# Projection stage of a hybrid backbone step: rotation tables and heads' Newton steps on GpSimd, half of the modulated tiles on ScalarE, pooling products one group sooner

## The chip, the cores and the metric

The kernel runs on one core of a Trainium2 chip. The metric is the device time of one execution in microseconds, as the median of several runs. The engines are called as in the profile: PE (TensorE, matrix products), PEld (its weight loads), DVE (VectorE), ACT (ScalarE), POOL (GpSimd) and SP (SyncE, which here only issues DMAs).

## What is computed

Two layers over 2048 latent tokens and 256 prompt tokens of width 1024. In each layer one input projection feeds three branches, attention, a short gated convolution and a multi-scale pooling, and one output projection joins them:

```python
xn = _rmsnorm(x, norm_g) * (1 + scl) + shift
proj = xn @ w_in
q, k, v, z_a, h_c, b_c, c_c, z_c, u_p, z_p = jnp.split(proj, SPLIT_IDX, axis=-1)
q = _rmsnorm(q.reshape(B, n, N_HEADS, HEAD_DIM), q_g)
k = _rmsnorm(k.reshape(B, n, N_KV_HEADS, HEAD_DIM), k_g)
...
q = _apply_rope(q, angs)
k_all = jnp.concatenate([_apply_rope(k, angs), ctx_k], axis=1)
...
attn = _attend(q, k_all, v_all) * jax.nn.silu(z_a)
conv = b_c * _short_conv(c_c * h_c, conv_w, conv_b) * jax.nn.silu(z_c)
pool = _pool_mix(u_p, pool_w, pool_scale) * jax.nn.silu(z_p)
out = jnp.concatenate([attn, conv, pool], axis=-1) @ w_out
return x + gate * out, k, v
```

The rotation applies to latent tokens alone; the prompt has none. `w_in` has 2816 columns: 512 of q, 128 of k, 128 of v, 512 of `z_a`, and six groups of 256.

## The kernel before

The kernel has two stages per layer: `phase_a`, the projection, and `phase_b`, attention and output projection. The change touches `phase_a` alone. It keeps about single precision by splitting each operand of a product into a rounded high part and the rest: `xh` and `xl` of the tokens, `wh` and `wl` of the weights, and three products for each, `wh*xh`, `wl*xh`, `wh*xl`. ACT makes the high parts by a cast; DVE and POOL share the low parts, a subtraction each (`split_w`, line 422: odd quarters of a weight tile on POOL, even ones on DVE).

The tokens of a layer are three blocks in the first half (two of 512 latent tokens and the prompt's 256) and two of 512 in the second. `norm_block` scales the tokens of a block by the root of their mean square. `tr_block` (line 431) transposes them on PE, eight tiles `trx` for the eight slices of the width; DVE makes of each the modulated tile `xf` (times `modA` plus `modB`), ACT the cast `xh`, POOL the difference `xl`. Only for the first block of layer 1 does ACT make every second `xf`. PE needs `xf` for the next transpose too, since two buffers hold the transposed tiles.

Over the blocks runs a sequence of weight tiles of 256 columns: two for q, one for kv, then the `rest` (z_a; h and c of the convolution; its b and z; u and z of the pooling), each as a loop over the blocks. While PE multiplies one tile, the next is split.

A q unit is 256 tokens times four heads. ACT copies the products to `raw` and squares them to `sq`, DVE sums the squares of each head to `hs` (line 500); POOL multiplies `raw` by the cosine table to `ra` (line 511), DVE by the sine table, four times into `sq` (line 520), and POOL adds both (line 181). When the block's last unit is there, `head_roots` (line 534) takes the inverse root of all `hs` of the block by three Newton steps, and `head_scale` (line 525, instruction on line 529) multiplies `ra` by it. Only then can PE transpose the heads (`trq`, `trk`), and ACT and DVE split them into `qh`, `ql` or `kh`, `kl`, which are stored. A block of 512 tokens has 16 roots per token row for q and 8 for kv; the prompt has half of them.

`newton_parts` (line 145) is a list of twelve instructions on DVE: `nt_v` (line 154), a shift `nt_t` (155) and a subtraction `nt_y` (157) on the bits as a start value, and then three times lines 151, 152 and 153. There are 15 of these for heads in each layer.

The rotation tables `trig` hold cosines and signed sines for 16 groups of 128 tokens. `small_loads` (line 375) multiplies them by the norm gains, once for q (g = 0) and once for k (g = 1), five instructions for each, all on DVE; in layer 0 it first multiplies `gains` by 8.

The pooling branch: `pool_out` sums windows on DVE (line 724 and on), ACT casts the difference to `dh`, POOL makes `dl`, and PE multiplies both with the group weights (`pmix`, lines 755 to 757). DVE scales the result to `po` (line 758), ACT casts it to `mh` and POOL subtracts `ml`, which are stored.

The order of instructions on each engine is written out by hand: every engine runs its queue in the order of the program, and waits are semaphores on tiles. Three helpers interleave work: `fine` runs one small function after every second k-slice of the products, `hook` runs after each unit, and `after(f, n)` (line 464) runs `f` at the n-th hook from now. The products of the pooling go through it:

```python
after(post, PR['po'])
```

`PR['po']` is 5. A hook is one unit on PE, 24 products of 512 columns for a latent block of the rest. `wg`, `wgh` and `wgl` are the split of the gated output weights, which fills the gaps of DVE, ACT and POOL in the later units.

Of the kernel before, what the change touches and what calls it, by code (L numbers as in the profile page):

```python
# [9 lines left out]
F32 = mybir.dt.float32  # L10
F32R = mybir.dt.float32r
F16 = mybir.dt.float16
I32 = mybir.dt.int32
# [17 lines left out]

PR = {'oa': 6, 'po': 5, 'q1': 3, 'q2': 5, 's0': 14, 's0p': 7, 'q1p': 0, 'ma': 3, 'mb': 1, 'd0': 3, 'd1': 2, 'dp': 1,
# [63 lines left out]
def hybrid_step(ctx: ExitStack, tc: tile.TileContext, A, O):  # L96
# [63 lines left out]
    def newton(pool, src, n, tag, eps):  # L160
        y, fns = newton_parts(pool, src, n, tag, eps)
        for f in fns:
            f()
        return y

    late = [[], []]
# [101 lines left out]
    def phase_a(l, xs_src, xp_src, nxt):  # L268


        with ExitStack() as st, ExitStack() as left:
# [102 lines left out]

            def small_loads():
                if l == 0:
                    nc.vector.tensor_scalar(out=gains, in0=gains, scalar1=8.0, scalar2=None, op0=ALU.mult)
                for g in range(2):
                    gn = gains[:, l, g:g + 1, :]
                    nc.vector.tensor_tensor(out=trig[:, g, 0], in0=trig[:, 1, 0], in1=gn.to_broadcast([128, 16, 64]),  # L380
                                            op=ALU.mult)
                    for c in range(2):
                        for f in range(2):
                            o, e = 32 * c + 16 * f, 32 * c + 16 * (1 - f)
                            nc.vector.tensor_tensor(out=trig[:, g, 1, :, o:o + 16], in0=trig[:, 1, 1, :, o:o + 16],
                                                    in1=gn[:, :, e:e + 16].to_broadcast([128, 16, 16]), op=ALU.mult)

# [42 lines left out]

            def tr_block(b, first=False):

# [5 lines left out]
                def one(k):  # L438
# [4 lines left out]
                    mA, mB = (m[:, l, k, b.cond:b.cond + 1] for m in (modA, modB))  # L443
                    if first and l and k % 2:
                        nc.scalar.activation(out=f[:, 0:b.n], in_=ps[:, 0:b.n], func=AF.Identity, scale=mA, bias=mB)
                    else:
                        nc.vector.tensor_scalar(out=f[:, 0:b.n], in0=ps[:, 0:b.n], scalar1=mA, scalar2=mB,
                                                op0=ALU.mult, op1=ALU.add)
# [85 lines left out]
            def head_roots(nh, b):  # L534
                m = b.n // 256 * 2 * nh
                b.r = newton(sm, b.ss[:, 0:m], m, "rh", 64 * EPS)

# [345 lines left out]
            for si, (half, kind, c) in enumerate(seq):  # L883
# [52 lines left out]
                def block(b, bi, kind, c, w):  # L936
# [10 lines left out]
                    elif kind == "za":  # L947
                        for m in range(2):
# [4 lines left out]
                            if si == 0 and (bi, m) == (1, 1):  # L953
                                if l:
                                    trig_loads()
                                    small_loads()
                                pool_loads()
# [43 lines left out]
                for bi, b in enumerate(order):  # L1001
                    if l == 0 and si == 0 and bi == 0:
                        fine.add([lambda i=i: split_w(w_next, i, 4) for i in range(4)])
                        nsplit[0] = 4
                        fine.add([lambda: norm_block(blocks[0][1]), small_loads])
                        fine.add([lambda: jobs_early.extend(jobs_at[1]())])
# [3 lines left out]
                        fns = [lambda i=i, f=f: (f(), others[i]() if i < len(others) else None)  # L1010
                               for i, f in enumerate(tr_block(blocks[0][1]))]
                        fine.add([lambda: None] * PR['e8'] + fns)
                        block(b, bi, seq[1][1], seq[1][2], w_next)
# [6 lines left out]
                    if si in (0, len(CH)) and bi + 1 < len(blocks[half]):  # L1020
                        fns = tr_block(blocks[half][bi + 1])
                        others = norm_parts(blocks[0][2]) if PR['np'] and l and si == 0 and bi == 0 else ()
# [806 lines left out]
```

## Time and profile before

| | us |
|---|---|
| median of 3 runs | 3221.98 (3221.13 to 3222.83) |
| the profiled execution | 3220.74 |
| its span, first to last instruction | 3219.0 |
| projection stage of layer 0 (with the start) | 0 to 672 |
| attention and output projection of layer 0 | 672 to 1620 |
| projection stage of layer 1 | 1620 to 2265 |
| attention and output projection of layer 1 | 2265 to 3219 |

The mean granted PE clock is 0.986 of full speed. In the rows, a time is the start in microseconds from the span's start, the number behind it how long it took (a row of several instructions has one sum), and a bracket at the end says how long the engine stood idle before and which instruction ended it. The profile's rows name shapes as partitions x elements. Matmuls overlap, so the distance of two starts is what one takes.

### The profile page before, as it was taken

The page shows a single profiled execution, that of the slowest core. Times are in us where ns is not written, and L with a number is a line of the kernel's source. Part 1 is how long each engine was busy: PE and PEld are TensorE (multiplying, and loading weights), DVE is VectorE, ACT ScalarE, POOL GpSimd, SP SyncE. Part 2 cuts the span into 40 slices and gives each one's busy share as a digit, 9 for nine tenths or more (in the row PEclk, how much of TensorE's full clock was granted, in tenths as well). Part 3 has the DMA queues.
Part 4 walks back from the last instruction along what each step waited for, and adds up shares of the span by engine and source line. Part 5 has one row for each costly group of instructions (what it writes and reads, how often), then busy time and mean ns, then how long its engine had stood idle before and what let it go on. Part 6 is the DMA issues. An engine that isn't in the chain of part 4 may idle for free.

```text
span 3219.0 us, 48084 instructions
## 1 busy us (share of the span) xinstructions
PE 3072.0 (95%) x17642; PEld 2438.0 (76%) x17642; DVE 2310.4 (72%) x3728; ACT 1833.5 (57%) x2634; POOL 2015.0 (63%) x1290
## 2 busy tenths in 40 slices
PE   6899999999999999999989999999899999999997
PEld 5788888766677777777769888988667777677775
DVE  5656575357888888888767555843778888888886
ACT  3323332237777777777742323331677887787785
POOL 2424462226888888888833334621578888898885
PEclk9999999999999999999999999999999999999999
DMA  7245744445234241323333455434623432342444
GB/s 249 90 129 188 246 143 136 131 132 156 74 120 119 62 128 56 105 79 110 127 138 100 148 165 193 131 99 120 171 80 117 123 102 76 90 132 83 130 145 149
DMA packets 371970, 408.40 MB, mean 127 GB/s; under 512 B 33428, under 2 KB 319640, under 8 KB 370968
## 3 DMA queue, kind: packets, MB, share of 16 engines
q1 hardware_dynamic: 371736, 405.33, 40.8%
q8 instruction: 140, 2.29, 0.3%
q14 instruction: 94, 0.77, 0.1%
HBM read 285.69 MB, written 119.55 MB: 126 GB/s over the span
## 4 chain that ended last, share of the span: by engine, by line
PE 69%; DVE 16%; ACT 4%; DMA 4%; issue 4%; POOL 2%; SPq 1%; DVEq 0%; ACTq 0%; POOLq 0%
PE mx L1158 7%; PE st L1198 6%; PE st L1197 6%; PE pv L1243 6%; PE rest L640 6%; PE rest L642 6%; PE rest L641 6%; PE pv L1250 4%; DVE mr L1159 4%; DVE Z L1229 3%; PE op L1376 3%; PE op L1377 3%; PE op L1378 3%; PE lc L1278 2%; PE qkv L481 2%
## 5 line engine op out<-in xcount | busy, mean ns | idle before, releaser
L181 POOL TENSOR_TENSOR pl<-P,ph 128x1024 f16<-128x1024 f32 (+2 forms) x594 | 1236.1, 2092 | 285.1 <-ACT ph L1209 256.6
L1159 DVE TENSOR_REDUCE mr<-mx 128x1 f32<-128x512 f32 x1024 | 696.2, 685 | 271.4 <-PE mx L1158 265.8
L1207 ACT ACTIVATE P<-st 128x1024 f32<-128x1024 f32 x576 | 636.0, 1104 | 286.3 <-PE st L1198 281.0
L1229 DVE TENSOR_REDUCE Z<-P 128x152 f32<-128x912 f32 (+2 forms) x576 | 695.7, 1208 | 6.6 <-ACT P L1207 5.5
L1209 ACT ACTIVATE ph<-st 128x1024 f16<-128x1024 f32 x584 | 591.3, 1012 | 0.0
L1158 PE MATMUL mx<-KH,T 128*128 128x512 f32 x1024 | 487.2, 477 | 34.5 <-DVE mr L1159 20.0
L640 PE MATMUL rest<-xh,wh 128*128 128x512 f32 (+1 forms) x1264 | 477.6, 378 | 2.2 <-ACT wh L427 2.2
L642 PE MATMUL rest<-xh,wl 128*128 128x512 f32 (+1 forms) x1264 | 469.3, 371 | 7.0 <-DVE wl L429 7.0
L641 PE MATMUL rest<-xl,wh 128*128 128x512 f32 (+1 forms) x1264 | 469.1, 371 | 2.0 <-POOL xl L181 2.0
L1197 PE MATMUL st<-T,KH 128*128 128x512 f32 x1152 | 462.5, 401 | 2.3 <-ACT ph L1209 2.3
L1198 PE MATMUL st<-T,KL 65*128 65x512 f32 x1152 | 460.4, 400 | 0.0
L1243 PE MATMUL pv<-ph,V 128*128 128x512 f16 x1152 | 351.3, 387 | 2.2 <-ACT P L1207 1.8
L1158 PEld LDWEIGHTS mx<-KH,T 128*128 128x128 f32 x1024 | 195.4, 191 | 195.2 <-DVE mr L1159 87.6
L429 POOL TENSOR_TENSOR wl<-wf,wh 128x512 fp32r<-128x512 f32 x88 | 124.0, 1409 | 277.8 <-ACT wh L427 256.7
L642 PEld LDWEIGHTS rest<-xh,wl 128*128 128x128 f32 x1264 | 240.3, 190 | 49.9 <-DVE wl L429 8.5
L640 PEld LDWEIGHTS rest<-xh,wh 128*128 128x128 f32 x1264 | 240.9, 191 | 46.2 <-issue 5.5
L641 PEld LDWEIGHTS rest<-xl,wh 128*128 128x128 f32 x1264 | 240.9, 191 | 40.4 <-POOL xl L181 3.3
L1198 PEld LDWEIGHTS st<-T,KL 65*128 65x128 f32 x1152 | 219.3, 190 | 48.0
L481 PE MATMUL qkv<-wl,xh 128*128 128x256 f32 x864 | 247.5, 287 | 7.2 <-DVE wl L429 4.2
L1197 PEld LDWEIGHTS st<-T,KH 128*128 128x128 f32 x1152 | 220.0, 191 | 41.3 <-ACT ph L1209 4.8
L480 PE MATMUL qkv<-wh,xh 128*128 128x256 f32 x864 | 250.9, 290 | 0.0
L482 PE MATMUL qkv<-wh,xl 128*128 128x256 f32 x864 | 246.5, 285 | 0.0
(234 smaller groups left out, 5533.8 us busy)
## 6 DMA issues: line engine op xcount, KB each, us to landing
wo<-woH SPq DMA_DIRECT2D x144, 256.0 KB, 3.7
wo<-woL SPq DMA_DIRECT2D x144, 256.0 KB, 5.1
wf<-in_w_in SPq DMA_DIRECT2D x50, 512.0 KB, 6.2
wa<-in_w_ada SPq DMA_DIRECT2D x24, 1024.0 KB, 6.7
wf<-in_w_in SPq DMA_DIRECT2D x19, 1024.0 KB, 5.6
woH<-wgh SPq DMA_DIRECT2D x64, 256.0 KB, 2.5
woL<-wgl SPq DMA_DIRECT2D x64, 256.0 KB, 2.5
T<-qH SPq DMA_DIRECT2D x128, 128.0 KB, 4.4
```

The source lines that it names most:

```text
L181: nc.gpsimd.tensor_tensor(out=out, in0=a, in1=b, op=op)
L640: nc.tensor.matmul(out=ps[:, 0:b.n], lhsT=wh[:, k, ms], rhs=b.h[:, k, :], start=(k == 0), stop=False)
L641: nc.tensor.matmul(out=ps[:, 0:b.n], lhsT=wh[:, k, ms], rhs=b.l[:, k, :], start=False, stop=False)
L642: nc.tensor.matmul(out=ps[:, 0:b.n], lhsT=wl[:, k, ms], rhs=b.h[:, k, :], start=False, stop=(k == KD - 1))
L1158: nc.tensor.matmul(out=ps, lhsT=u.T1[:, q * 128:(q + 1) * 128], rhs=u.KH[u.g][:, c * 512:(c + 1) * 512])
L1159: nc.vector.reduce_max(out=mr[:, q, c:c + 1], in_=ps, axis=AX.X)
L1197: nc.tensor.matmul(out=ps[:, i, :], lhsT=u.KH[u.g][:, kt], rhs=u.T1, start=True, stop=False)
L1198: nc.tensor.matmul(out=ps[:, i, :], lhsT=u.KL[u.g][0:65, kt], rhs=u.T2, start=False, stop=True)
L1207: nc.scalar.activation(out=P, in_=ps, func=AF.Exp, scale=0.125)
L1209: nc.scalar.activation(out=ph, in_=ps, func=AF.Exp, scale=0.125)
L1229: nc.vector.tensor_reduce(out=z[:, c], in_=u.P[grp][:, 0:ns, c, :].rearrange("p s n t -> p n s t"), axis=AX.XY, op=ALU.add)
L1243: nc.tensor.matmul(out=u.po, lhsT=u.V[u.g][:, 2 * j + i, :], rhs=ph[:, i, :], start=(j == 0 and i == 0), stop=False)
```

## The change

Four edits, all of `phase_a`:

1. `small_loads` takes the half g and its instructions go to POOL. In layer 0 the first half stays where the whole stood (behind the norm of block 1), the second goes behind the transposes of block 1. In layer 1 the first half stays and the second comes four hooks later.
2. `head_roots` uses `newton_gp`: the three start instructions stay on DVE (with the scale 1.0 in the first), the three steps are four POOL instructions each. It holds for the 15 Newtons of the heads in each layer; the norm of the tokens keeps the old one.
3. In layer 0, blocks 1 and 2 of the first half have every second `xf` made by ACT (`beside`).
4. `PR['po']` is 4: the pooling products come one hook sooner.

DVE has 299 instructions fewer, POOL 381 more, ACT 8 more; PE has the same.

```diff
-PR = {'oa': 6, 'po': 5, 'q1': 3, 'q2': 5, 's0': 14, 's0p': 7, 'q1p': 0, 'ma': 3, 'mb': 1, 'd0': 3, 'd1': 2, 'dp': 1,
+PR = {'oa': 6, 'po': 4, 'q1': 3, 'q2': 5, 's0': 14, 's0p': 7, 'q1p': 0, 'ma': 3, 'mb': 1, 'd0': 3, 'd1': 2, 'dp': 1,
...
+    def newton_gp(pool, src, n, tag, scale, eps):
+
+        v = pool.tile([128, n], F32, tag="nt_v", name="nt_v")
+        y = pool.tile([128, n], F32, tag=tag, name="nt_y")
+        t = pool.tile([128, n], F32, tag="nt_t", name="nt_t")
+        ps, ts = nc.gpsimd.tensor_scalar, nc.vector.tensor_scalar
+        step = [lambda: padd(t, y, y, ALU.mult), lambda: padd(t, t, v, ALU.mult),
+                lambda: ps(out=t, in0=t, scalar1=-0.5, scalar2=1.5, op0=ALU.mult, op1=ALU.add),
+                lambda: padd(y, y, t, ALU.mult)]
+        return y, [lambda: ts(out=v, in0=src, scalar1=scale, scalar2=eps, op0=ALU.mult, op1=ALU.add),
+                   lambda: ts(out=t.bitcast(I32), in0=v.bitcast(I32), scalar1=1, scalar2=None,
+                              op0=ALU.logical_shift_right),
+                   lambda: ts(out=y.bitcast(I32), in0=t.bitcast(I32), scalar1=-1.0, scalar2=float(0x5F3759DF),
+                              op0=ALU.mult, op1=ALU.add)] + step * 3
...
-            def small_loads():
-                if l == 0:
-                    nc.vector.tensor_scalar(out=gains, in0=gains, scalar1=8.0, scalar2=None, op0=ALU.mult)
-                for g in range(2):
-                    gn = gains[:, l, g:g + 1, :]
-                    nc.vector.tensor_tensor(out=trig[:, g, 0], in0=trig[:, 1, 0], in1=gn.to_broadcast([128, 16, 64]),
-                                            op=ALU.mult)
-                    for c in range(2):
-                        for f in range(2):
-                            o, e = 32 * c + 16 * f, 32 * c + 16 * (1 - f)
-                            nc.vector.tensor_tensor(out=trig[:, g, 1, :, o:o + 16], in0=trig[:, 1, 1, :, o:o + 16],
-                                                    in1=gn[:, :, e:e + 16].to_broadcast([128, 16, 16]), op=ALU.mult)
+            def small_loads(g):
+
+                if l == 0 and g == 0:
+                    nc.gpsimd.tensor_scalar(out=gains, in0=gains, scalar1=8.0, scalar2=None, op0=ALU.mult)
+                gn = gains[:, l, g:g + 1, :]
+                padd(trig[:, g, 0], trig[:, 1, 0], gn.to_broadcast([128, 16, 64]), ALU.mult)
+                for c in range(2):
+                    for f in range(2):
+                        o, e = 32 * c + 16 * f, 32 * c + 16 * (1 - f)
+                        padd(trig[:, g, 1, :, o:o + 16], trig[:, 1, 1, :, o:o + 16],
+                             gn[:, :, e:e + 16].to_broadcast([128, 16, 16]), ALU.mult)
...
-                    if first and l and k % 2:
+                    if (l and first or not l and beside) and k % 2:
                         nc.scalar.activation(out=f[:, 0:b.n], in_=ps[:, 0:b.n], func=AF.Identity, scale=mA, bias=mB)
...
-                b.r = newton(sm, b.ss[:, 0:m], m, "rh", 64 * EPS)
+                b.r, fns = newton_gp(sm, b.ss[:, 0:m], m, "rh", 1.0, 64 * EPS)
+                for f in fns:
+                    f()
...
                                 if l:
                                     trig_loads()
-                                    small_loads()
+                                    small_loads(0)
+                                    after(lambda: small_loads(1), 4)
                                 pool_loads()
...
-                        fine.add([lambda: norm_block(blocks[0][1]), small_loads])
+                        fine.add([lambda: norm_block(blocks[0][1]), lambda: small_loads(0)])
...
-                               for i, f in enumerate(tr_block(blocks[0][1]))]
-                        fine.add([lambda: None] * PR['e8'] + fns)
+                               for i, f in enumerate(tr_block(blocks[0][1], beside=True))]
+                        fine.add([lambda: None] * PR['e8'] + fns + [lambda: small_loads(1)])
...
-                        fns = tr_block(blocks[half][bi + 1])
+                        fns = tr_block(blocks[half][bi + 1], beside=not si)
```

In the changed file the lines from 163 on stand 15 to 17 further down: `head_scale` is 543, `xf` 461, the rotation's product 525, `padd` 196, `po` 774.

**DVE, layer 0, the first q Newton and what follows it** (a row is line, operation, output <- inputs, shape, count). Before, from the last sine products to the prompt's tiles:

```order
L520 TENSOR_TENSOR sq<-raw,trig 128x8x16 x4
L154 TENSOR_SCALAR nt_v<-hs 128x16
L155 TENSOR_SCALAR nt_t<-nt_v 128x16
L157 TENSOR_SCALAR nt_y<-nt_t 128x16
L151 SCALAR_TENSOR_TENSOR nt_t<-nt_y 128x16
L152 TENSOR_TENSOR nt_t<-nt_t,nt_v 128x16
L153 SCALAR_TENSOR_TENSOR nt_y<-nt_t,nt_y 128x16
...
L529 TENSOR_TENSOR ra<-ra,nt_y 128x512 x2
L447 TENSOR_SCALAR xf<-trx,modA,modB 128x256 x8
```

Now:

```order
L534 TENSOR_TENSOR sq<-raw,trig 128x8x16 x4
L175 TENSOR_SCALAR nt_v<-hs 128x16
L176 TENSOR_SCALAR nt_t<-nt_v 128x16
L178 TENSOR_SCALAR nt_y<-nt_t 128x16
L543 TENSOR_TENSOR ra<-ra,nt_y 128x512 x2
L461 TENSOR_SCALAR xf<-trx,modA,modB 128x256 x4
```

The nine steps are gone from this queue, `head_scale` follows the start value directly, and four of the prompt's eight tiles have left.

**POOL, the same place.** Before, from the last unit's rotation on:

```order
L511 TENSOR_TENSOR ra<-raw,trig 128x512
L181 TENSOR_TENSOR ra<-ra,sq 128x512
L181 TENSOR_TENSOR xl<-xf,xh 128x256 x8
L391 MEMSET pwf 128x128 x2
L511 TENSOR_TENSOR ra<-raw,trig 128x512
```

Now:

```order
L525 TENSOR_TENSOR ra<-raw,trig 128x512
L196 TENSOR_TENSOR ra<-ra,sq 128x512
L196 TENSOR_TENSOR nt_t<-nt_y 128x16
L196 TENSOR_TENSOR nt_t<-nt_t,nt_v 128x16
L173 TENSOR_SCALAR nt_t<-nt_t 128x16
L196 TENSOR_TENSOR nt_y<-nt_y,nt_t 128x16
...
L196 TENSOR_TENSOR trig<-trig,gains 128x1024
L196 TENSOR_TENSOR trig<-trig,gains 128x16x16 x4
L196 TENSOR_TENSOR xl<-xf,xh 128x256 x8
```

Twelve small steps and then five table rows stand between the rotation's sum and the prompt's `xl`. In the other Newtons no table follows, but the rows that followed the sum before: a `wl`, a rotation, or the prompt's gains.

**DVE, layer 1, the first pooling unit.** Before, from its scaling on:

```order
L740 SCALAR_TENSOR_TENSOR s<-s,kc,rb 128x256
L429 TENSOR_TENSOR wl<-wf,wh 128x512
L758 SCALAR_TENSOR_TENSOR po<-pmix,cols,rb 128x508 x2
L429 TENSOR_TENSOR wl<-wf,wh 128x512
L689 COPY carry<-rb 128x16 x2
```

Now:

```order
L756 SCALAR_TENSOR_TENSOR s<-s,kc,rb 128x256
L774 SCALAR_TENSOR_TENSOR po<-pmix,cols,rb 128x508 x2
L443 TENSOR_TENSOR wl<-wf,wh 128x512 x2
L774 SCALAR_TENSOR_TENSOR po<-pmix,cols,rb 128x256
L705 COPY carry<-rb 128x16 x2
```

The scaling of the products stands ahead of both quarters of the weight tile instead of between them, and that of the prompt ahead of the second pooling unit.

## Rows read from the trace of the kernel before

**Rows 1.** The page's busy time by engine, share of the span, instructions

```profile
PE 3072.0 (95%) x17642; PEld 2438.0 (76%) x17642; DVE 2310.4 (72%) x3728; ACT 1833.5 (57%) x2634; POOL 2015.0 (63%) x1290
```

**Rows 2.** Windows: us, busy us of PE, PEld, DVE, ACT, POOL, clock, DMA, GB/s

```profile
0.00:672.00 672.00, 620.63 (x3854) 529.52 (x3854) 367.77 (x784) 200.25 (x370) 243.64 (x207) 0.98 0.52 165
...
1620.00:2265.00 645.00, 616.53 (x3566) 538.96 (x3565) 379.56 (x733) 207.81 (x382) 241.63 (x203) 0.98 0.43 135
```

**Rows 3.** PE's timeline: start, us, engine, line, tiles, [idle before <-releaser]

```profile
71.66 0.90 PE L441 MATMUL trx<-kc,x 128*128 128x128 f32 x3 [5.35 <-DVE xf L447]
...
94.55 0.44 PE L441 MATMUL trx<-kc,x 128*128 128x128 f32 x2 [2.98 <-DVE xf L447]
...
148.66 0.85 PE L230 MATMUL aps<-wa,sT 128*32 128x256 f32 x12 [2.22 <-DVE ql L558]
...
486.01 1.08 PE L230 MATMUL aps<-wa,sT 128*32 128x256 f32 x8 [3.68 <-DVE ql L558]
...
1758.12 0.63 PE L551 MATMUL trq<-kc,ra 128*128 128x128 f32 x4 [1.58 <-DVE ra L529]
```

**Rows 4.** The windows of two stretches of 4 us, columns as in group 2

```profile
72.00:76.00 4.00, 4.00 (x22) 4.00 (x21) 2.04 (x6) 3.38 (x7) 3.42 (x4) 0.54 0.02 4
92.00:96.00 4.00, 1.45 (x9) 1.22 (x10) 3.76 (x11) 1.33 (x4) 0.99 (x2) 1.00 0.00 0
```

**Rows 5.** DVE's timeline ahead of the wait of 5.35 us

```profile
62.83 0.29 DVE L377 TENSOR_SCALAR gains<-gains 128x256 f32<-128x256 f32 x1
...
69.21 0.67 DVE L500 TENSOR_REDUCE hs<-sq 128x8 f32<-128x512 f32 x1
```

**Rows 6.** POOL's timeline in the same stretch

```profile
64.53 1.33 POOL L511 TENSOR_TENSOR ra<-raw,trig 128x512 f32<-128x512 f32 x1 [8.60 <-DVE trig L380]
```

**Rows 7.** DVE's timeline, one 16-wide heads' Newton and `head_scale`

```profile
142.00 0.17 DVE L154 TENSOR_SCALAR nt_v<-hs 128x16 f32<-128x16 f32 x1
...
142.61 1.28 DVE L151 SCALAR_TENSOR_TENSOR nt_t<-nt_y 128x16 f32<-128x16 f32 x1
143.93 1.22 DVE L152 TENSOR_TENSOR nt_t<-nt_t,nt_v 128x16 f32<-128x16 f32 x1
...
146.71 1.29 DVE L529 TENSOR_TENSOR ra<-ra,nt_y 128x512 f32<-128x512 f32 x2
```

**Rows 8.** POOL's timeline beside that Newton

```profile
143.82 1.30 POOL L429 TENSOR_TENSOR wl<-wf,wh 128x512 fp32r<-128x512 f32 x1
```

**Rows 9.** POOL's timeline, small dependent steps in the last stage

```profile
3182.74 0.20 POOL L181 TENSOR_TENSOR nt_t<-or 128x4 f32<-128x4 f32 x1
...
3184.69 0.20 POOL L181 TENSOR_TENSOR or<-or,nt_t 128x4 f32<-128x4 f32 x1
```

**Rows 10.** POOL's timeline, long subtractions of the pooling branch

```profile
268.97 2.65 POOL L181 TENSOR_TENSOR dl<-s,dh 128x1016 fp32r<-128x1016 f32 x1 [6.48 <-ACT dh L744]
...
1831.31 2.34 POOL L181 TENSOR_TENSOR dl<-s,dh 128x1016 fp32r<-128x1016 f32 x1 [3.92 <-ACT dh L744]
...
1859.24 2.37 POOL L181 TENSOR_TENSOR dl<-s,dh 128x1016 fp32r<-128x1016 f32 x1 [7.94 <-ACT dh L744]
...
1880.24 2.34 POOL L181 TENSOR_TENSOR ml<-po,mh 128x1016 fp32r<-128x1016 f32 x1
```

**Rows 11.** PE's timeline at the first products of three pooling units

```profile
275.93 0.40 PE L755 MATMUL pmix<-dh,pwh 128*128 128x508 f32 x1
276.17 0.40 PE L756 MATMUL pmix<-dl,pwh 128*128 128x508 f32 x1
...
1833.70 0.50 PE L756 MATMUL pmix<-dl,pwh 128*128 128x508 f32 x1 [1.87 <-POOL dl L181]
...
1863.73 0.39 PE L756 MATMUL pmix<-dl,pwh 128*128 128x508 f32 x1
```

**Rows 12.** PE's timeline, two waits in a weight split

```profile
1880.59 0.50 PE L640 MATMUL rest<-xh,wh 128*128 128x512 f32 x1 [1.24 <-ACT wh L427]
...
1883.19 0.50 PE L642 MATMUL rest<-xh,wl 128*128 128x512 f32 x1 [1.87 <-DVE wl L429]
```

More of the change, by code (lines that the diff above doesn't have):

```diff
@@ L429, in split_w, with tr_block @@
                 eng.tensor_tensor(out=lo[:, s], in0=v, in1=h[:, s], op=ALU.subtract)
-            def tr_block(b, first=False):
+            def tr_block(b, first=False, beside=False):
                 nt = b.n // 128
```

## The prediction, made blind

> **What bounds the kernel now.** I read the page first: TensorE (PE) is busy for 95% of the span, VectorE (DVE) for 72%, GpSimd (POOL) for 63% [rows 1]. So a gain must come out of PE's idle time, or out of a clock that is not granted, in the stretches that the change touches. Those are the two projection stages, one per layer. In the windows by stage PE is busy 620.63 of 672 us in the first and 616.53 of 645 us in the second [rows 2]; the first includes the start-up, which the change leaves alone. Then I read PE's timeline there for rows with an idle time, and the engine behind each. They are short and have a pattern: PE waits 5.35 us for `xf` from DVE, 2.98 us for `xf`, 2.22 and 3.68 us for `ql`, 1.58 us for `ra` [rows 3], and each time DVE had just run either the rotation tables or a heads' Newton. Last come the timelines of DVE and POOL at these places.
>
> **Tables of layer 0.** DVE makes them in one go: `gains` starts at 62.83, and the next work, the sum `hs`, at 69.21 [rows 5]: 6.4 us in which the tiles `xf` that PE needs stand behind them. POOL is idle for 8.60 us until 64.53 [rows 6], so its first half of the tables fits there. The price on POOL: a 128x1016 subtraction takes 2.34 us [rows 10], a 128x512 one 1.30 [rows 8], so 128x1024 about 2.4 and 128x256 about 0.65, by estimate; a half of the tables is 2.4 + 4 x 0.65 = 5.0 us. They are not free for DVE: ahead of 62.83 it runs the small steps of the token norm and the scaling of x, and a DVE instruction that meets a POOL one waits to its end (two steps of the 0.17-us kind take 1.28 and 1.22 beside POOL's work [rows 7]). In the worst case the norm meets all five POOL rows and is put off by some 4 of their 5 us, and the gain on DVE is only 6.4 - 4 = 2.4. In the best case the whole stall of 5.35 goes, and with it the clock: the granted clock is 0.54 from 72 to 76 and 1.00 again at 92 to 96, right after a stall of 2.98 [rows 4], so 4 x (1 - 0.54) = 1.8 us more, 7.2 in all. A middle value is nearer the best, as POOL has 8.60 us for 5.0: **-6**. What is late next is `xl`, which POOL makes from these tiles; that does not change.
>
> **The second half of the tables** is put behind the first Newton on POOL, ahead of the prompt's eight `xl`, and DVE's two `head_scale` (line 529, 1.29 us for both [rows 7]) are ready at the moment when POOL starts a 2.4-us table. If POOL starts first, DVE waits 2.4 us, then 0.65 behind a small one, and the prompt's `xf`, for which PE already waits 2.98 us, come that much later: 3.1, and with the Newton's own delay (below) more. If DVE starts first it is 0. POOL has no semaphore to wait for there, so I take the first: **+3.5** (0 to 5). In layer 1 the same block stands ahead of a `wl` and an `ra`. PE has no idle time there before, so some of it is slack: **+1** (0 to 4.5). The tables that DVE gives up in layer 1 lie where PE does not wait: 0. The eight `xf` that go to ScalarE are 0 too: it is mostly idle there, and PE waits for the first tile, which stays on DVE.
>
> **Newton.** Before: three start steps and nine small steps on DVE, of 0.17 us where nothing is in their way (the first [rows 7]). At 142.00 the whole thing takes 4.71 us to `head_scale` at 146.71, of which 2.1 are two waits for POOL's `ra` and `wl` [rows 7]. After: three steps on DVE, then twelve on POOL. POOL's small dependent steps exist once in this trace, in the last stage: from 3182.74 to 3184.69 lie seven intervals [rows 9], 1.95 / 7 = 0.28 us each; twelve are 3.35. (Those are 128x4, these 128x16: at 0.20 us most of a step is not the elements.) The third start step ends with POOL's `ra` in any case (that wait of about 1.2 stays), so a 16-wide Newton takes about 0.5 + 1.2 + 3.35 + 0.1 = 5.1 us from start to `head_scale`, against 4.71 here. DVE's order has `head_scale` right behind the third start step, so DVE is not free for other work meanwhile: 299 instructions fewer, but the queue stands. Behind the last Newton step POOL has a `wl` ready (1.30 [rows 8]) that ran *during* the Newton before; started first, it holds `head_scale` for 1.3 us. So the site costs 0.4 to 1.7 us. There are some eight such sites where PE already waits behind a Newton; four are shown [rows 3]. At 0.7 each: **+5.5** (0 to 12).
>
> *A rule of the Trainium skill against the trace.* The rows above show that two steps of 0.17 us took as long as the POOL instruction beside them. "SBUF — State Buffer", section "Who interferes with whom", says that VectorE and GpSimd hold one port pair exclusively for a whole instruction, whoever starts first; the trace agrees. By the same skill's "GPSIMD Engine Reference", section "Engine selection", elementwise work on two inputs belongs on VectorE, being about 2x slower on GpSimd, which speaks against this change; by that factor the nine steps of 0.17 would be 3.1 us, where the rows give 3.35 for twelve, so the sum stays.
>
> **Pooling products one group sooner.** A group is 24 matmuls at 0.23 to 0.24 us from start to start [rows 11], 5.6 us. In layer 1 PE already waits 1.87 us for `dl` at the first one [rows 11], whose POOL instruction runs from 1831.31 to 1833.65 [rows 10]; nothing in the change makes that chain earlier. So PE comes 5.6 us sooner and waits 7.5: +5.6 and a clock drop of 1.8, **+7.4**. At the next one PE reads `dl` (done 1861.61) from 1863.73 on; 5.6 sooner it would wait 3.5, less about 2, since `po` and `wl` in front of that chain also come sooner: +1.6. In layer 0 the same: `dl` done at 271.62, read at 276.17 [rows 10, 11]: 5.6 - 4.55 = +1. In return `po`, `mh`, `ml` come before the split of the next weight tile and no longer between its parts. Before, `ml` (2.34 us from 1880.24 [rows 10]) held DVE's `wl`, and PE waited 1.24 and 1.87 us [rows 12], followed by slower matmuls worth about as much as the drop above: -4.9. Sum 7.4 + 1.6 + 1 - 4.9, **+5** (0 if the chain gives way by as much, 11 if the return stays out).
>
> **The sum** is -6 + 3.5 + 1 + 5.5 + 5 = +9 us, against the profiled execution of 3220.74 us (span 3219.0): 3229.7. That execution stands 1.2 us under the median of 3221.98, so the forecast is 3231. With all terms at their lower ends it is -7.2, so 3215; at their upper ends -2.4 + 5 + 4.5 + 12 + 11 = +30, so 3252.
>
> **The rivals.**
> - *Faster: a quick hand-back.* Place: the end of each Newton. If DVE's `head_scale` starts ahead of POOL's next instruction, and the POOL steps hide the waits that DVE had within the Newton (1.28 + 1.22 at 142 [rows 7]), a site goes from 4.7 to 4.4 or less. It decides from 4.4 us on, counted from the first Newton step to `head_scale`: then Newton and tables cost nothing (0 for +3.5, +1, +5.5), the tables give 7.2, and `dl`, behind a less crowded DVE, is some 4 us sooner, so the products cost 1: -6 to -10, about **3214**. For it: DVE is the releaser of nearly all of PE's waits here. Against it: `head_scale` stands directly behind the start steps.
> - *No difference.* The change shifts waits from one engine to the other without changing when `head_scale` ends (in this sense it does not do what it says), and 0 for Newton and +3 for the products meet -6 and +3.5: **3222**.
> - *GpSimd becomes the bound.* POOL's `wl` halves come 3.35 us later at each Newton and 5 us more behind the tables. If PE waits for those as it does for DVE's, every term is at its upper end: **3248**.
>
> **How the numbers follow.** Forecast, slower by about 9: 0.38. GpSimd as the bound: 0.08. No difference: 0.27. Faster: 0.27. A measurement of this kernel tells 0.2%, 6.4 us, from no change; so faster 0.27, same 0.27, slower 0.46. The range runs from 3212, just under the faster rival's 3214, to 3246, just under the bound one's 3248; what is left out is a gain of over 10 us (0.1) and the bound case (0.08).
>
> **What would show it.** In the changed kernel's profile: PE's wait of 5.35 near 71 us gone or under 3 (tables); PE's wait before the prompt's transposes over 5 us, with POOL on a 128x1024 table during it (second half); `head_scale` some 5 us after the first Newton step and over 1 us long where a `wl` runs on POOL; a wait of 6 to 8 us for `dl` at the first product of layer 1, and none near 1880. It would be wrong if the products' chain in layer 1 is sooner than now, or if DVE gets to `head_scale` first: then the time falls under 3222.

## The result and the profile after

| | before | after |
|---|---|---|
| median of 4 runs each, us | 3221.56 (3220.26 to 3222.83) | 3269.27 (3266.92 to 3275.66) |
| ratio of the times, 95% interval | | 1.0153 (1.0140 to 1.0165) |
| the profiled execution and its span | 3220.74, 3219.0 | 3266.92, 3265.1 |
| mean granted PE clock | 0.986 | 0.979 |

The change costs 47.7 us. The forecast was 3231, the range 3212 to 3246: the sign was right, the size was five times too small, and the range missed it.

The page's busy time of the changed kernel, columns as in [rows 1], and the windows by stage, columns as in [rows 2]; the last two windows are of 4 us each.

```profile
PE 3088.1 (95%) x17642; PEld 2450.9 (75%) x17642; DVE 2271.2 (70%) x3429; ACT 1838.2 (56%) x2642; POOL 2117.1 (65%) x1671
```

```profile
0.00:697.00 697.00, 626.05 (x3855) 532.76 (x3856) 349.33 (x633) 204.69 (x378) 293.79 (x398) 0.97 0.51 159
1644.00:2281.00 637.00, 598.11 (x3439) 524.35 (x3439) 339.75 (x558) 202.91 (x372) 293.32 (x393) 0.97 0.42 132
...
96.00:100.00 4.00, 2.48 (x8) 2.09 (x9) 1.96 (x4) 2.44 (x6) 4.00 (x6) 0.50 0.00 0
...
504.00:508.00 4.00, 3.02 (x21) 1.75 (x22) 3.97 (x12) 0.00 (x0) 0.78 (x1) 0.50 0.30 98
```

DVE is busy for 39 us less and POOL for 102 us more [rows 1], and yet the time rises. The whole loss lies in the two projection stages. That of layer 0 ends at 697 instead of 672 us; that of layer 1 takes 637 us instead of 615. The second stage of layer 0 takes 947 us (697 to 1644), before 950 (672 to 1622). For layer 1 the old kernel's window with the same 3439 matmuls is this:

```profile
1622.00:2237.00 615.00, 587.29 (x3439) 515.51 (x3439) 359.42 (x703) 202.64 (x372) 241.63 (x203) 0.98 0.43 137
```

So in layer 1 PE stands idle for 637.0 - 598.1 = 38.9 us instead of 615.0 - 587.3 = 27.7, and the same matmuls take 10.8 us longer. In layer 0 the idle time goes from 672 - 620.6 = 51.4 to 70.9 us [rows 2], the busy time up by 5.4. Of the 47 us, 31 are waits and 16 are matmuls that take longer. The granted clock is 0.50, the lower of its two levels, in the stretches right after the two longest waits (96:100 and 504:508, above). Behind the first of these it was 1.00 before, at 92 to 96 [rows 4]. Behind the second it had been 0.50 before the change too, so this drop is not new; the window of the old kernel:

```profile
486.00:490.00 4.00, 3.99 (x26) 2.72 (x27) 3.97 (x10) 0.00 (x0) 1.74 (x2) 0.50 0.43 133
```

New ones stand behind shorter waits: 0.64 at 134 to 138, 0.63 at 158 to 162 and 0.61 at 537 to 541, where the same work had 1.00 before (128.5 to 132.5, 148.7 to 152.7, 516.3 to 520.3).

PE's timeline of the changed kernel, the rows that answer to [rows 3, 11]:

```profile
64.60 0.47 PE L455 MATMUL trx<-kc,x 128*128 128x128 f32 x1 [4.39 <-DVE x L339]
...
97.52 0.69 PE L455 MATMUL trx<-kc,x 128*128 128x128 f32 x2 [7.35 <-DVE xf L461]
...
157.98 1.07 PE L245 MATMUL aps<-wa,sT 128*32 128x256 f32 x16 [3.72 <-DVE ql L574]
...
504.98 1.93 PE L245 MATMUL aps<-wa,sT 128*32 128x256 f32 x16 [7.01 <-DVE ql L574]
...
1754.14 1.12 PE L567 MATMUL trq<-kc,ra 128*128 128x128 f32 x4 [4.74 <-DVE ra L543]
...
1793.18 0.63 PE L567 MATMUL trq<-kc,ra 128*128 128x128 f32 x4 [4.13 <-DVE ra L543]
...
1870.90 0.49 PE L771 MATMUL pmix<-dh,pwh 128*128 128x508 f32 x1 [3.50 <-ACT dh L760]
1873.32 0.79 PE L772 MATMUL pmix<-dl,pwh 128*128 128x508 f32 x1 [1.92 <-POOL dl L196]
```

The waits that stood behind a Newton have grown: 2.98 to 7.35, 2.22 to 3.72, 3.68 to 7.01, 1.58 to 4.13. The same matmuls are later by 3.0, 9.3, 19.0 and 35.1 us: the lateness adds up from one to the next. The 5.35 us at 71 are gone, with a new wait of 4.39 at 64.60 in front of them.

What happens at one Newton is seen on DVE and POOL at the place that [rows 7] shows. DVE's timeline, then POOL's:

```profile
149.81 0.17 DVE L175 TENSOR_SCALAR nt_v<-hs 128x16 f32<-128x16 f32 x1
...
150.22 1.16 DVE L178 TENSOR_SCALAR nt_y<-nt_t 128x16 int32<-128x16 int32 x1
155.00 2.33 DVE L543 TENSOR_TENSOR ra<-ra,nt_y 128x512 f32<-128x512 f32 x2 [3.61 <-POOL nt_y L196]
```

```profile
150.06 1.29 POOL L196 TENSOR_TENSOR ra<-ra,sq 128x512 f32<-128x512 f32 x1 [1.12 <-DVE nt_v L175]
151.47 0.22 POOL L196 TENSOR_TENSOR nt_t<-nt_y 128x16 f32<-128x16 f32 x1
...
154.74 0.22 POOL L196 TENSOR_TENSOR nt_y<-nt_y,nt_t 128x16 f32<-128x16 f32 x1
154.92 1.26 POOL L443 TENSOR_TENSOR wl<-wf,wh 128x512 fp32r<-128x512 f32 x1
```

The twelve small steps take 154.92 - 151.47 = 3.45 us. DVE stands idle for 3.61 us, since `head_scale` is next in its queue and waits for the last step. POOL's `wl` starts at 154.92, DVE's `head_scale` at 155.00: POOL is first by 0.08 us, and the pair of `head_scale` takes 2.33 us instead of 1.29. It is the same at 19 of the 30 Newtons, all those at which POOL has a product, a subtraction or a table ready: each of these starts ahead of `head_scale` by 0.08 us. From the first Newton step to the end of `head_scale` DVE spends 5.19 + 2.33 = 7.5 us, before 4.71 + 1.29 = 6.0.

The groups by line show the sum of it. Of the kernel before (busy us, mean ns | idle before), then of the changed kernel:

```profile
L529 DVE TENSOR_TENSOR ra<-ra,nt_y 128x512 f32<-128x512 f32 (+1 forms) x48 | 28.8, 639 | 1.8
L529 DVE TENSOR_TENSOR raw<-raw,nt_y 128x512 f32<-128x512 f32 (+1 forms) x6 | 3.6, 603 | 0.6
```

```profile
L543 DVE TENSOR_TENSOR ra<-ra,nt_y 128x512 f32<-128x512 f32 (+1 forms) x48 | 55.6, 1197 | 85.1 <-POOL nt_y L196 81.7 <-POOL rb L700 3.4
L543 DVE TENSOR_TENSOR raw<-raw,nt_y 128x512 f32<-128x512 f32 (+1 forms) x6 | 4.7, 783 | 20.5 <-POOL nt_y L196 20.5
```

`head_scale` is busy for 60.3 us instead of 32.4, and DVE stands idle for 105.6 us in front of it. That idle time takes the place of the nine steps that left DVE; summed over the 30 Newtons, first step to start of `head_scale`, DVE needs 142.7 us where it needed 118.3. Together 24.4 + 27.9 = 52 us more on DVE's queue, for a kernel that is 47.7 slower.

### The profile page after: what moved, and what is told of

The parts are those of the page before. It is cut to its first block, busy times and chain, and to the rows that moved or that the text cites. A ratio compares the mean times of both kernels' runs of the same rounds, so it can differ in the third digit from the quotient of the medians.

```text
span 3265.1 us, 48156 instructions
## 1 busy us (share of the span) xinstructions
PE 3088.1 (95%) x17642; PEld 2450.9 (75%) x17642; DVE 2271.2 (70%) x3429; ACT 1838.2 (56%) x2642; POOL 2117.1 (65%) x1671
```

## The experiments

The theory: the loss is the Newton edit; DVE is held at every Newton, first by the wait for POOL's steps, then by POOL's next instruction, and what is queued behind `head_scale` comes late. The rivals: the tables on POOL, the pooling products or ACT's tiles cost it; or GpSimd is simply too slow for what is put on it. Each run is compared with runs of the kernel before on its own chip (medians 3221.0, 3223.4 and 3224.0 us for the three groups of runs).

**One edit undone.** `e1_newton_dve` is the changed kernel with the Newton on DVE:

```diff
-                b.r, fns = newton_gp(sm, b.ss[:, 0:m], m, "rh", 1.0, 64 * EPS)
-                for f in fns:
-                    f()
+                b.r = newton(sm, b.ss[:, 0:m], m, "rh", 64 * EPS)
```

> The changed kernel with the heads' Newton back on DVE, everything else as changed. Theory T (each edit has its own cost, and PE's delay at each place in the two timelines adds up): the Newton sites hold about 28 of the 47 us, so some 3241 us, about 20 over the kernel before, with the waits of 7.35 (prompt's transposes) and 4.74 us (first trq of layer 1 behind the second tables) still there, if somewhat smaller. Rival R (crowding: it is the sum of tables and Newton on POOL that makes either expensive): 3222 to 3230. Rival P (the products one group sooner are what costs): over 3260.

Measured: 3229.56, ratio 1.0029 (1.0017 to 1.0041). Nearly the whole loss is gone with this edit. The time is under the 3241 expected. A part of the remaining 8.5 us is seen where POOL's second half of the tables meets a Newton, now on DVE. The timelines of that kernel, DVE's and POOL's:

```profile
94.11 2.32 DVE L151 SCALAR_TENSOR_TENSOR nt_t<-nt_y 128x16 f32<-128x16 f32 x1
96.46 0.64 DVE L152 TENSOR_TENSOR nt_t<-nt_t,nt_v 128x16 f32<-128x16 f32 x1
```

```profile
94.00 5.10 POOL L196 TENSOR_TENSOR trig<-trig,gains 128x1024 f32<-128x1024 f32 x5
```

Five small DVE steps last as long as the five table instructions beside them, and this Newton takes 7.47 us (3.48 before). In layer 1 the first Newton meets the other second half and takes 9.79 us (5.59 before).

`e2_tables_dve` is the changed kernel with the tables back on DVE, in one go:

```diff
-                padd(trig[:, g, 0], trig[:, 1, 0], gn.to_broadcast([128, 16, 64]), ALU.mult)
+                    nc.vector.tensor_tensor(out=trig[:, g, 0], in0=trig[:, 1, 0], in1=gn.to_broadcast([128, 16, 64]),
+                                            op=ALU.mult)
...
-                        fine.add([lambda: norm_block(blocks[0][1]), lambda: small_loads(0)])
+                        fine.add([lambda: norm_block(blocks[0][1]), small_loads])
```

> The changed kernel with the rotation tables back on DVE in one go, as before; Newton on POOL, ScalarE's tiles and the products one group sooner stay. Theory T: the second half of the tables holds about 15 us (7 in layer 0, 8 in layer 1), the first half about 0, so some 3254 us; the wait near 71 us comes back and the one of 7.35 falls to about 4.5. Rival R: 3230 or less. Rival P: over 3260.

Measured: 3267.24, 1.0148 (1.0127 to 1.0168). Not to be told from the changed kernel, where 3254 was expected: beside the Newton on POOL, no cost of the tables can be told. The first rival falls.

**One edit alone.** `e5_newton_only` is the kernel before with the Newton on POOL (the diff of `e1`, reversed):

> The kernel before with the heads' Newton on POOL alone. Theory T: each 16-wide Newton takes about 5.2 us to head_scale and head_scale then waits behind a wl where one is ready; 28 us in all, so some 3250. Rival R: without the tables on POOL the Newtons cost under 8, below 3230.

Measured: 3263.70, 1.0136 (1.0114 to 1.0159), 42.7 us. That is more than either case expected, and it rules out that only tables and Newton together make the loss. The same groups and the same wait are there without the other three edits; the group by line, and PE's timeline:

```profile
L544 DVE TENSOR_TENSOR ra<-ra,nt_y 128x512 f32<-128x512 f32 (+1 forms) x48 | 52.4, 1130 | 85.1 <-POOL nt_y L196 81.7 <-POOL rb L701 3.4
```

```profile
503.93 1.94 PE L245 MATMUL aps<-wa,sT 128*32 128x256 f32 x16 [7.01 <-DVE ql L575]
```

In this kernel the first step of the first Newton (`nt_v`, at 89.27 before) is 0.4 us late, that of the fifteenth and last of layer 0 (at 526.42 before) 24.0 us: 1.7 us more with each Newton in the mean, and only once, ahead of the seventh, is a part made up (1.0 us). In layer 1 the fifteen go from 20.9 to 37.2 us late. (The profiled execution is the fastest of the four, 3255.74 us; PE ends 35 us late in it.)

`e6_po4_only` is the kernel before with the products one hook sooner (`'po': 5` to `'po': 4`):

> The kernel before with the pooling products one hook sooner alone. Theory T: about +1 in layer 0, +7 at the first product of layer 1, and -10 behind it (the weight split near 1880 and a later one near 1968): 3220, within 0.2% of before. The prediction's own term was +5: 3227. Rival P: over 3240.

Measured: 3220.27, 1.0005 (0.9992 to 1.0019): no difference. PE's timeline of that kernel shows the wait that the forecast names:

```profile
1827.65 0.79 PE L755 MATMUL pmix<-dh,pwh 128*128 128x508 f32 x1 [5.07 <-ACT dh L744]
1830.07 0.79 PE L756 MATMUL pmix<-dl,pwh 128*128 128x508 f32 x1 [1.62 <-POOL dl L181]
```

But the two waits near 1880 [rows 12] are gone, and a later one of 3.95 us for a `wl`, near 1968, is 1.27 us. Against the kernel before, PE is 4.5 us early at 1750, 6.3 us late right after the first product and 6.7 us early at 1973. (The profiled execution, 3210.45 us, is the fastest of the ten, and the first 4.5 us of its lead lie ahead of the products of layer 1.)

`e4_acts_only` is the kernel before with ACT's tiles (`beside`), and `e8_acts_po4` has these and the sooner products:

```diff
-                    if first and l and k % 2:
+                    if (l and first or not l and beside) and k % 2:
                         nc.scalar.activation(out=f[:, 0:b.n], in_=ps[:, 0:b.n], func=AF.Identity, scale=mA, bias=mB)
```

> The kernel before with ScalarE's second tiles in layer 0 alone. The prediction put them at 0. In the trace of the kernel with these and the products, PE came 3 us later between 79 and 97 us. If that is theirs: 3223 to 3226, and the timeline shows xh behind xf on ScalarE. If it is chance: 3221 within 2.

> The kernel before with ScalarE's tiles and the products one hook sooner, Newton and tables as before. Products alone were 3220 against 3221; the ScalarE tiles were put at 0. So 3215 to 3222. It prices the tables on POOL: the kernel with all but the Newton moved was 3229.6; the difference, some 10 us, is theirs. If it comes out at 3229 too, the tables cost nothing and ScalarE's tiles are what costs.

Measured: 3225.70, 1.0008 (0.9997 to 1.0019), and 3224.56, 1.0003 (0.9993 to 1.0014). Neither can be told from no change. In `e4`'s trace PE does wait 2.17 us for an `xf` at 79.44, where it waited 0.59 before, but the time does not tell 1.6 us from noise. The difference of `e1` to `e8` is the tables on POOL alone: 1.0029 against 1.0003, some 8 us by these two ratios.

`e7_dve_split_late` adds to `e8` the tables on DVE, but in two halves, the second five hooks later (four in layer 1):

```diff
-                        fine.add([lambda: norm_block(blocks[0][1]), small_loads])
+                        fine.add([lambda: norm_block(blocks[0][1]), lambda: small_loads(0)])
...
+                        after(lambda: small_loads(1), 5)
```

> As the one with ScalarE's tiles and the products sooner, but the tables on DVE in two halves: the first where it stands, the second five hooks later in layer 0 (behind the prompt's tiles) and four hooks later in layer 1. About 3 us of the wait of 5.35 us near 71 us and its clock drop of 1.8 go: 3210 to 3218. If POOL's rows had been the only fault of the split, this shows it; if the wait near 71 us stays, the norm of the tokens is what holds the tiles, not the tables.

Measured: 3222.05, 0.9997 (0.9986 to 1.0009). PE's wait near 71 is halved, and its timeline shows a wait of 3.19 us behind the second Newton all the same, where the kernel before had 2.97 at 128.49; no gain can be told, where 3210 to 3218 was expected.

```profile
68.54 1.12 PE L455 MATMUL trx<-kc,x 128*128 128x128 f32 x4 [2.88 <-DVE xf L461]
...
126.94 0.58 PE L495 MATMUL qkv<-wl,xh 128*128 128x256 f32 x1 [3.19 <-DVE wl L443]
```

**Chain or hold?** The lateness at a Newton has two parts, the longer chain and the slower `head_scale`. `e10_one_step` is `e5` with one Newton step of the three (two left out):

```diff
-                for f in fns:
+                for f in fns[0:7]:
```

> The kernel before with the heads' Newton on POOL and one step of the three (it leaves out the other two, so the roots are rough): four POOL rows in place of twelve, 2.4 us less per Newton. The handing over to POOL and back and POOL's next row ahead of head_scale stay. If the length of the chain is what costs, about as before or faster, 3205 to 3225 (from start to head_scale 2.8 us against 4.5 before). If handing over and the held head_scale cost (23 us of the 48 that DVE was later in all), 3235 to 3245.

Measured: 3207.02, 0.9951 (0.9936 to 0.9966). Its `head_scale` is as slow as in `e5`; the group by line, then DVE's and POOL's timelines:

```profile
L544 DVE TENSOR_TENSOR ra<-ra,nt_y 128x512 f32<-128x512 f32 (+1 forms) x48 | 51.7, 1117 | 30.1 <-POOL nt_y L196 27.8 <-POOL rb L701 2.3
```

```profile
148.30 2.37 DVE L544 TENSOR_TENSOR ra<-ra,nt_y 128x512 f32<-128x512 f32 x2 [1.22 <-POOL nt_y L196]
```

```profile
148.22 1.30 POOL L444 TENSOR_TENSOR wl<-wf,wh 128x512 fp32r<-128x512 f32 x1
```

The sum from the first step to `head_scale` is 73.3 us, 45 less than before, and `head_scale` 55.3, 22.9 more: 22 us less on DVE's queue, and 16.4 us are measured. In `e5` the same count is 24.4 + 23.6 = 48 us more, and 42.7 measured. Counted by the chain alone, 24.4 us more would cost 42.7 and 45 less would gain only 16.4; with both parts, 0.89 and 0.75 us of time go with each microsecond on DVE's queue. So by this sum both parts count. No run takes the slower `head_scale` away and leaves it on DVE.

**Taking the hold away.** If DVE is held because `head_scale` stands in its queue behind POOL's steps, moving that one instruction to POOL should give the loss back, although POOL then does still more. `e11_change_scale_pool` is the changed kernel with it, `e9_scale_pool` is `e5` with it, and `e12_scale_pool_po4` is `e9` with `'po': 4`:

```diff
-                nc.vector.tensor_tensor(
+                nc.gpsimd.tensor_tensor(
                     out=av, in0=av,
```

> The changed kernel with one edit more: head_scale on POOL. Theory H (DVE's queue that stands at head_scale is what cost): most of the 47 us goes and the gain of the Newton comes: 3204.6 (Newton and scaling on POOL alone) plus some 8 for the tables on POOL and ScalarE's tiles, 3205 to 3216. Rival (POOL is full once it has tables, Newton and scaling): over 3230.

> The kernel before with the heads' Newton and head_scale on POOL: DVE has only the three start steps and goes on at once. In the Newton on POOL alone, head_scale on DVE started 5.2 us after the first step (16 wide) and was held by POOL's next rows up to 3.4 us. Theory H (what costs is that DVE's queue stands: wl, ql and xf behind head_scale come late): DVE's waits go, POOL has two rows of about 1.3 us more per Newton; 3215 to 3230. Rival C (what costs is the long chain itself: heads ready late for their transposes, POOL's own wl late): as slow as the Newton on POOL alone, 3250 to 3275.

> Newton and head_scale on POOL with the products one hook sooner, tables and tiles as before. The products alone were worth 0 to 2 us, so 3200 to 3206; PE's waits of 1.10 and 1.88 near 1863 us and of 3.43 near 1951 us go, a longer one for dl comes at the first product of layer 1.

Measured: `e11` 3220.72, 0.9994 (0.9983 to 1.0004); `e9` 3204.58, 0.9945 (0.9930 to 0.9960); `e12` 3209.98, 0.9957 (0.9943 to 0.9971). One instruction turns the change's +47.7 into no difference, and `e5`'s +42.7 into -18.8. `e9` is faster than both its cases, `e11` and `e12` are slower than expected (3205 to 3216, 3200 to 3206). Beside `head_scale` on POOL the change's other three edits together thus cost half a per cent (`e11` against `e9`, 0.9994 against 0.9945), which no run divides among them. POOL is busy for 2143.6 us in `e9`, more than in the changed kernel's 2117.1, so POOL's load was not the trouble there. DVE's timeline of `e9`, then POOL's:

```profile
121.86 1.17 DVE L178 TENSOR_SCALAR nt_y<-nt_t 128x16 int32<-128x16 int32 x1
122.95 0.68 DVE L444 TENSOR_TENSOR wl<-wf,wh 128x512 fp32r<-128x512 f32 x1
```

```profile
127.06 2.04 POOL L544 TENSOR_TENSOR ra<-ra,nt_y 128x512 f32<-128x512 f32 x2
129.06 1.26 POOL L444 TENSOR_TENSOR wl<-wf,wh 128x512 fp32r<-128x512 f32 x1
```

DVE goes on to the next `wl` right behind the start value, 4 us before `head_scale` even starts. `e12` and `e9` have intervals that overlap; whether the sooner products cost something there stays open.

**The Newton back on DVE, `head_scale` alone on POOL.** `e13_newton_dve_scale_pool` is the kernel before with only the edit above:

> The kernel before with only head_scale on POOL, Newton on DVE. It tells the two apart: if the scaling alone makes the gain, 3203 to 3208 as with both; if the steps on POOL do their part, DVE still has nine steps and their waits (4.5 us in the mean from the first step on), gains only the 1.3 us of the scaling at each site and whatever held it: 3210 to 3218.

Measured: 3197.56, **0.9928 (0.9913 to 0.9942)**: 26.4 us faster than the kernel before, under both ranges expected, and the lowest time of all, though its interval overlaps that of `e9`. Its page, then the timelines of DVE and POOL at the Newton that was just shown for `e9`, and of PE:

```profile
PE 3066.5 (96%) x17642; PEld 2436.7 (76%) x17642; DVE 2289.0 (72%) x3674; ACT 1833.6 (57%) x2634; POOL 2066.1 (65%) x1344
```

```profile
120.10 0.17 DVE L154 TENSOR_SCALAR nt_v<-hs 128x16 f32<-128x16 f32 x1
...
123.39 0.18 DVE L153 SCALAR_TENSOR_TENSOR nt_y<-nt_t,nt_y 128x16 f32<-128x16 f32 x1
123.48 0.69 DVE L429 TENSOR_TENSOR wl<-wf,wh 128x512 fp32r<-128x512 f32 x1
```

```profile
123.65 2.42 POOL L529 TENSOR_TENSOR ra<-ra,nt_y 128x512 f32<-128x512 f32 x2 [2.00 <-DVE nt_y L153]
126.03 1.26 POOL L429 TENSOR_TENSOR wl<-wf,wh 128x512 fp32r<-128x512 f32 x1
```

```profile
92.86 0.44 PE L441 MATMUL trx<-kc,x 128*128 128x128 f32 x2 [1.67 <-DVE xf L447]
...
127.35 0.39 PE L481 MATMUL qkv<-wl,xh 128*128 128x256 f32 x1 [2.07 <-POOL wl L429]
```

The whole Newton takes 3.38 us on DVE here. POOL waits 2.00 us for it, and its `wl`, queued behind `head_scale`, can no longer run beside DVE's steps; in the kernel before it did, and two of the steps took 1.28 and 1.22 us [rows 7]. DVE does its own `wl` at once. PE's waits of 2.22, 3.68 and 1.58 us for `ql` and `ra` [rows 3] are not in its timeline any more. POOL needs 2.0 to 2.5 us for what DVE did in 1.29, and it still pays.

The four kernels together give the price of the hold. With `head_scale` on DVE, the Newton on POOL costs 42.7 us (`e5`); with `head_scale` on POOL it costs 7.6 (-18.8 in `e9` against -26.4 in `e13`, intervals that overlap). So some 35 of the 42.7 us come only where the scaling waits in DVE's queue. The 26.4 us of `e13` are a gain of its own: how much of it is DVE's shorter work and how much its freer queue, no run separates, and leaving `head_scale` on DVE but behind the next `wl` was not tried.

## Why the prediction was right or wrong

**What bounds the kernel** was read rightly: PE, by short waits behind DVE in the projection stages. All of the loss lies there.

**Newton, +5.5: the step that failed**, measured 42.7 alone. The site was worked out rightly: 5.1 us from start to `head_scale` were forecast, 5.16 to 5.20 measured for 16 columns; POOL's `wl` first and `head_scale` over 1 us longer (of the sixteen pairs of 16 columns in the changed kernel six take 2.3 to 2.4 us, eight, with two POOL instructions or a table in the way, 3.4 to 4.0, and two, with nothing in the way, 1.3). Three things went wrong in the sum:

- The price of a site was put at 0.7, between 0.4 and 1.7. Over all 30 it is 48 / 30 = 1.6 (`e5`), at the upper end. The 4.71 us at 142 that the forecast started from are close to the mean of the sixteen Newtons of 16 columns (3.48 to 5.71), so their chain grew by 0.45 only. But the fourteen smaller ones, where POOL was mostly not in DVE's way before, went from 3.05 to 4.28 in the mean, and the forecast did not look at them.
- Only "some eight sites" were counted, those where PE already waits. But DVE's lateness goes from one Newton to the next, 1.7 us each in the mean in layer 0 of `e5`: what a Newton without a wait loses is paid at the next wait. Thirty sites at 1.6 would have given 48.
- No clock was counted for these waits, though it was for the tables and the products. Of the 24 us that PE is late at the end of layer 0's Newtons in `e5`, its idle time accounts for 15 (from 56 us on, over the same 2914 matmuls, 26.9 us before and 42.1 after); the rest is matmuls that take longer. The clock was granted 0.50 to 0.64 in the 4 us behind five waits of 2.95 to 4.89 us, where it had been 1.00; behind the wait of 7.01 us nothing is added, since it had been 0.50 there.

The upper end of this term, 12, had the same count of eight in it. So it was no bound, and with it the range was too narrow.

**Tables, first half, -6.** The wait at 71 is gone, as forecast, but PE's lead over the old kernel is 2.5 us just before the tables (55 to 61) and 1.4 after (86 to 91): no gain is left. (ACT's tiles fall into the same stretch, and PE waits 1.52 us for an `xf` at 77.71, where it waited 0.59.) The trace took the worst case that the prediction names, the token norm behind POOL's five rows. DVE's and POOL's timelines of the changed kernel:

```profile
56.54 1.84 DVE L332 TENSOR_SCALAR ms<-ss 128x4 f32<-128x4 f32 x1 [2.80 <-ACT junk L328]
58.41 0.67 DVE L154 TENSOR_SCALAR nt_v<-ms 128x4 f32<-128x4 f32 x1
...
61.20 1.19 DVE L152 TENSOR_TENSOR nt_t<-nt_t,nt_v 128x4 f32<-128x4 f32 x1
...
63.79 2.74 DVE L339 TENSOR_SCALAR x<-x,nt_y 128x1024 f32<-128x1024 f32 x4
...
93.08 3.93 DVE L543 TENSOR_TENSOR ra<-ra,nt_y 128x512 f32<-128x512 f32 x2 [3.62 <-POOL nt_y L196]
```

```profile
55.92 5.22 POOL L196 TENSOR_TENSOR trig<-trig,gains 128x1024 f32<-128x1024 f32 x5
...
93.00 5.96 POOL L196 TENSOR_TENSOR trig<-trig,gains 128x1024 f32<-128x1024 f32 x5
```

The norm's steps last 63.79 - 56.54 = 7.25 us, before 2.58 (57.59 to 60.17): 4.7 us, close to the "4 of their 5" of the worst case. The value "nearer the best" was a choice against a row: POOL's idle time, 8.60 us to 64.53 [rows 6], begins at 55.93, ahead of the norm, so the tables had to fall on it.

**Tables, second half, +3.5 and +1.** The mechanism was right: POOL starts first (93.00 against 93.08), `head_scale` takes 3.93 us, PE waits 7.35 (over 5 was forecast), and the clock falls to 0.50. PE goes from 1.4 early to 4.5 late there, 5.9 us, of which the Newton alone has 3.2 (`e5`, 0.4 to 3.6 late at the same matmuls). So some 2.7 us are left for the 3.5 forecast. In layer 1, where the tables met slack by the forecast, PE waits 4.74 us for `trq` at 1754 and loses 4.6 us more than in `e5` over the same matmuls (1715 to 1765): the 1 forecast was too small. Alone, without Newton on POOL, the tables cost some 8 us (`e1` against `e8`), where the two halves together were forecast at -1.5.

**Products, +5.** The wait for `dh` and `dl` at the first one in layer 1 is there, 3.50 + 1.92 = 5.4 us for the 7.5 forecast, and none is left near 1880. The return was sized too small: it reaches past 1883, to the wait near 1968. Measured alone: no difference.

**ACT's tiles, 0.** No difference can be told in `e4` and `e8`, so the 0 stands as far as is known.

**The rivals.** The quick hand-back fails at its own condition: POOL's next instruction starts ahead of `head_scale`, by 0.08 us, at every Newton of the changed kernel where POOL has such an instruction ready. GpSimd as the bound, at 3248 (3252 with the first term at its upper end too, as in the forecast's own sum), is the nearest in time, but not in mechanism: PE waits for DVE's tiles, and the kernels in which POOL has more to do (`e9`, `e11`) are faster. None of the cases had the lateness carried from Newton to Newton. The cause itself stands in the prediction ("DVE is not free for other work meanwhile: 299 instructions fewer, but the queue stands"), but without a price.

*The rule on engines.* That `head_scale` is faster on POOL's queue goes against the duration of the instruction, 1.29 us on DVE, 2.0 to 2.5 on POOL. The Trainium skill, "GPSIMD Engine Reference", section "4.1 Engine selection", puts elementwise work on two inputs on VectorE, with GpSimd about 2x slower. The rows give 1.6 to 1.9, near that factor; the runs do not agree on the choice at this place, since `e13` is 0.72% faster.

## What to carry to other kernels

Moving a short chain to another engine frees nothing if the instruction behind it in the old queue waits for the chain's end: count the idle time in front of that instruction as work, at every place where it stands, and not only where the bounding engine waits today, since lateness is carried on to the next wait. Ask which instruction ends the chain and move that one first: here the last multiplication alone, slower on its new engine, gave 0.72%, and the nine steps in front of it without it cost 1.4%. Before the steps are put beside another engine's queue, look which of its instructions is ready at the moment of the hand-over; it went first at every such place here.

## What was not expected of the hardware

- POOL's next ready instruction starts before the DVE instruction that its last step releases: 154.92 against 155.00, 148.22 against 148.30, 93.00 against 93.08. The first instruction of DVE's pair then ends some 0.55 us after it, and the pair takes 2.3 to 4.0 us instead of 1.29. Where DVE starts first, POOL's instruction is the one that lasts: in `e5` DVE's `head_scale` starts at 1753.67 and takes its usual 0.69 us, and the 128x512 product that POOL starts at 1753.81 takes 1.68 instead of 1.29. The Trainium skill, "SBUF — State Buffer", section "Who interferes with whom", says that whoever starts first holds the pair; the rows agree, and add who starts first at a hand-over of this kind.
- A dependent small step on POOL takes 0.20 to 0.22 us and comes every 0.28 (128x8) to 0.30 us (128x16), where DVE's come every 0.20 to 0.21: twelve of 128x16 on POOL are 3.45 us, nine on DVE alone 1.9.
- The length of a wait alone does not tell the clock behind it. The windows right behind PE's waits of 7.35 and 7.01 us were granted 0.50, and that behind 2.98 us before the change 1.00 [rows 4]; but behind 3.68 us before the change it was 0.50 (486 to 490), and in `e5` 0.50 behind 2.95 us (196.2 to 200.2).
